# A two-layer encoder: the Fourier branch folded by the symmetry of its channel transform, and the tokens reordered for block copies

## The chip, the cores and the metric

One core of one Trainium2 chip runs the whole kernel in one launch. The metric is the device time of one execution in microseconds (us). The kernel before took 1846.51 us (median of three runs, 1846.41 to 1850.01). Its profile is of one execution whose span, from the first to the last recorded instruction, is 1841.9 us.

## What is computed

Two layers over 512 tokens of 1024 channels, all in float32. Each layer is a SwiGLU half-step, a mixer and a second SwiGLU half-step; the mixer is where the change lies:

```python
# mixer, h = RMSNorm(x)
z = h @ w_in                      # q, k, v (8 heads x 64), uf (512), ga, gf (1024 each)
y_na = neighbourhood_attention(q, k, v, rpb) @ w_na_out
y_f = fourier_mix(uf) @ w_f_out
g_na = jax.nn.sigmoid(ga + gate_bias[0])
g_f = jax.nn.sigmoid(gf + gate_bias[1])
return (g_na * y_na + g_f * y_f) @ w_o

def fourier_mix(u):               # real part of a 2-D DFT, per channel group
    ug = u.astype(jnp.float32).reshape(B, T, F_GROUPS, F_GROUP_DIM)   # 4 groups x 128
    f = jnp.fft.fft2(ug, axes=(1, 3), norm="ortho").real
    return f.reshape(B, T, F_WIDTH).astype(u.dtype)
```

The input of the transform is real. So F(k, c), the result at position frequency k and channel c, equals F(-k, -c), with -k taken modulo 512 and -c modulo 128. The attention sees an 8 x 64 grid of tokens; queries in a block of 16 columns attend to a band of 32 columns in all 8 rows.

## The kernel before, in words

TensorE (PE) multiplies float32 numbers that were split into a high and a low part, each held as fp32r: a product is three matmuls, high by high, high by low and low by high (`mm3`, L326 to L328; `late_low`, L521, L522, L524, for the block products). Weights stream in granules of 128 x 1024 (512 KB). SyncE (SP) issues a load for each (L148); where a granule is the sum of two, either GpSimd (POOL) issues a second, accumulating DMA once the first has landed (L158) or VectorE (DVE) adds the two (L172). ScalarE (ACT) then writes the high part (`whi`; L199, L194, or L179 in `prep_high`) and DVE the low part (`wlo`; L202, L195, L183). The large products are done by Strassen's seven products (`strassen`, `product`), in which a granule feeds twelve matmuls with 512 columns of weights each.

The mixer is `stage_mixer`. It projects u, v, q and k; for the Fourier branch it makes the position transform (`four_pos`), a rotation on DVE (`rotated`), the split of the result (`high_of`), the channel transform (`four_ch`, 24 matmuls for two groups), its assembly into 512 positions (`four_q` on ACT, L1287; `four_y` on DVE, L1292) and its split (`four_high`: ACT L1306, DVE L1310). `rows_of` then multiplies the transform by `w_f_out`: for each of two column halves i and each of four token tiles, four channel groups by three matmuls, 96 in all in a layer. `f_copy` moves a result to SBUF (DVE L1561, once ACT L1559). At the end of the mixer `fill` does the same for the attention's output with `w_na_out`, and the gate blocks begin (`gate_block`, whose first products need the granules that the raw pool opened by `swap_pools(0)` has room for).

Attention goes by eight units (`Probs`, p0 to p7), a head pair and two query blocks each: `att_scores` (PE L1342), `maxes` (DVE L1358), `exps` (ACT L1367), `inverse` (DVE L1370), `scaled` (ACT L1375), `transposed` (PE L1383), `kept` (ACT L1393), `att_pv` (PE L1409), `att_split` (ACT L1418, DVE L1419). The matmuls of the Fourier branch are laid between the units, so that PE works while ACT and DVE do the softmax. In the mixer the order on DVE and ACT is the order in which the code is written (`manual_schedule`), as it stands in the last 150 lines of `stage_mixer`, and the trace shows the instructions of an engine start in that order. The DMA instructions of SP and POOL stand in queues of their own, whose order a scheduler lays down; in the trace they are issued in that order. `minus` (DVE L1548, L1550) and the lines behind it (L1754 to L1769, `t`) prepare the operands of the first gate products.

Of the kernel before, what the change touches and what calls it, by code (L numbers as in the profile page):

```python
# [9 lines left out]
F32 = mybir.dt.float32  # L10
# [24 lines left out]
UNIT = (0, 1, 4, 5, 7, 6, 3, 2)  # L35
KEYS = ((0, 6), (2, 5), (2, 4), (1, 6))

# [5 lines left out]
def _granules():  # L43
# [7 lines left out]
    for l in range(L):  # L51
        for w in (1, 2):
# [15 lines left out]
            if w == 1:  # L68
# [4 lines left out]
                for name, n in (("qk", 8), ("f", 4)):  # L73
                    for g in range(n):
                        put(s, name, g)
# [16 lines left out]
def encoder_kernel(  # L92
# [67 lines left out]
    class Item:  # L160
        def __init__(self, raw, add=None, neg=False, stage=0, parts=1, pieces=1, then=None):
            self.raw, self.add, self.neg, self.stage, self.parts = raw, add, neg, stage, parts
            self.pieces, self.then = pieces, then
# [6 lines left out]
        def summed(self):  # L170
            if self.add:
                V.tensor_tensor(self.raw.t, self.raw.t, self.add.t, ALU.add)  # L172
                self.add = None

        def prep_high(self):

            n, t = self.raw.n, self.raw.t
# [31 lines left out]
    def stage_items():  # L209
# [52 lines left out]
        for l in range(L):  # L262
# [6 lines left out]
            for key in qk[5:] + [(s, "f", g) for g in range(4)]:  # L269
                add(Raw(key))  # L270
            st += 1
# [839 lines left out]
    def stage_mixer(l, norm, nxt):  # L1111
# [5 lines left out]
        ch = mp.tile([P, 2, 2, P], F32R, tag="ch", name=nm("ch"), bufs=1)  # L1117
# [3 lines left out]
        G.dma_start(out=ch, in_=chan)  # L1121
        dfs, rots = [], []
# [13 lines left out]
        def proj_T(scale, ahead=AHEAD, hook=None):  # L1136
            ps = bank()
            wh, wl = ws.next(ahead)
            for kt in range(DT):
# [3 lines left out]
                mm3(ps, wh[:, c], wl[:, c], *xs[kt], kt == 0, kt == DT - 1)  # L1143

            def out(now=True):

                t = tmp(s="q")
                V.tensor_tensor(t, ps, R, ALU.mult)
# [31 lines left out]
        vt = [None] * TB  # L1180

        def value(b, src):
            vt[b] = slot(F32, "v", (T,))
# [93 lines left out]
        def four_ch(b):  # L1277
            bh, bl = b
            p1, p2 = bank(), bank()
            mm3(p1[:, 0:258], ch[:, 0, 0, :], ch[:, 0, 1, :], bh[:, 0:258], bl[:, 0:258], True, True)  # L1280
            mm3(p2[:, 0:256], ch[:, 1, 0, :], ch[:, 1, 1, :], bh[:, 256:512], bl[:, 256:512], True, True)
            return p1, p2

        def four_q(p2):
            qs = tmp(s="fq")
            V.memset(qs[:, 0:1], 0.0)
            S.activation(qs[:, 1:256], p2[:, 1:256], AF.Copy)  # L1287
            return qs

        def four_y(p1, qs):  # L1290
            y = tmp(s="fy")
            V.tensor_tensor(y[:, 0:256], p1[:, 0:256], qs[:, 0:256], ALU.subtract)  # L1292
# [773 lines left out]
```

## Time and profile before

| | before |
|---|---|
| median of the runs | 1846.51 us |
| span of the profiled execution | 1841.9 us |
| around that span, to the median | 4.6 us |
| matrix work (PE) | 1832.5 us busy, 99% of the span |
| DVE busy | 1602.0 us, 87% |
| ACT busy | 1316.5 us, 71% |
| POOL busy | 175.8 us, 10% |
| moved by DMA | 396.77 MB, mean 215 GB/s |

The profile's page counts busy time by engine; a busy PE can be one whose matmuls follow each other without a gap, and 99% says that little time is left in which PE stands. The timeline gives each instruction's start, length, line, output and inputs, with in brackets how long the engine had been idle before it and what released it. The windows view gives the busy time of each engine in a stretch. In the trace the attention of the first layer lies between about 398 and 473 us, that of the second between about 1312 and 1387 us.

### The profile page before, as it was taken

The page shows a single profiled execution, that of the slowest core. Times are in us where ns is not written, and L with a number is a line of the kernel's source. Part 1 is how long each engine was busy: PE and PEld are TensorE (multiplying, and loading weights), DVE is VectorE, ACT ScalarE, POOL GpSimd, SP SyncE. Part 2 cuts the span into 40 slices and gives each one's busy share as a digit, 9 for nine tenths or more (in the row PEclk, how much of TensorE's full clock was granted, in tenths as well). Part 3 has the DMA queues.
Part 4 walks back from the last instruction along what each step waited for, and adds up shares of the span by engine and source line. Part 5 has one row for each costly group of instructions (what it writes and reads, how often), then busy time and mean ns, then how long its engine had stood idle before and what let it go on. Part 6 is the DMA issues. An engine that isn't in the chain of part 4 may idle for free.

```text
span 1841.9 us, 24538 instructions
## 1 busy us (share of the span) xinstructions
PE 1832.5 (99%) x8834; PEld 1528.6 (83%) x8834; DVE 1602.0 (87%) x1942; ACT 1316.5 (71%) x1781; POOL 175.8 (10%) x215
## 2 busy tenths in 40 slices
PE   9999999999999999999999999999999999999998
PEld 7888888888888888888888888888888888888886
DVE  7878899886989988889998888997869899888898
ACT  6777875668676767787667777766686776777865
POOL 0010011100111010001010100101001101010010
PEclk9999999999999999999999999999999999999999
DMA  9898798933887799879888987998258877988795
GB/s 304 224 236 221 186 278 268 227 121 118 238 228 188 157 237 244 215 202 267 250 200 210 237 215 194 280 310 193 69 175 214 231 192 175 230 214 221 206 286 156
DMA packets 202538, 396.77 MB, mean 215 GB/s; under 512 B 108016, under 2 KB 108144, under 8 KB 202416
## 3 DMA queue, kind: packets, MB, share of 16 engines
q1 hardware_dynamic: 173072, 295.28, 51.3%
q0 software_dynamic: 28912, 99.38, 29.5%
q8 instruction: 69, 1.13, 0.2%
q10 hardware_dynamic: 432, 0.55, 0.1%
q14 instruction: 53, 0.43, 0.1%
HBM read 367.88 MB, written 2.11 MB: 201 GB/s over the span
## 4 chain that ended last, share of the span: by engine, by line
PE 99%; DVE 0%; ACT 0%; DMA 0%; issue 0%
PE A L521 10%; PE A L524 10%; PE A L522 10%; PE o L521 8%; PE o L522 8%; PE o L524 8%; PE B L521 5%; PE B L522 5%; PE B L524 5%; PE ps L326 4%; PE ps L327 3%; PE ps L328 3%; PE C L522 3%; PE C L521 3%; PE C L524 3%; PE tr L433 1%
## 5 line engine op out<-in xcount | busy, mean ns | idle before, releaser
L202 DVE TENSOR_TENSOR wlo<-raw,whi 128x1024 fp32r<-128x1024 f32 (+1 forms) x532 | 628.4, 1192 | 168.4 <-ACT whi L199 166.2
L199 ACT ACTIVATE whi<-raw 128x1024 fp32r<-128x1024 f32 (+1 forms) x532 | 545.0, 1034 | 262.3 <-DVE raw L172 56.2
L158 POOL DMA_DIRECT2D raw<-in_wst_dram x166 | 145.3, 901 | 1279.1 <-DMA raw<-in_wst_dram 519.8
L172 DVE TENSOR_TENSOR raw<-raw,raw 128x1024 f32<-128x1024 f32 (+1 forms) x148 | 176.4, 1192 | 2.0
L522 PE MATMUL A<-whi,xl 128*128 128x512 f32 x400 | 155.7, 389 | 0.0
L521 PE MATMUL A<-whi,xh 128*128 128x512 f32 x400 | 155.7, 389 | 0.0
L376 ACT ACTIVATE at<-zt 128x1024 uint16<-128x1024 uint16 (+2 forms) x96 | 110.3, 1166 | 12.7 <-DMA zt<-zs 12.7
L524 PE MATMUL A<-wlo,xh 128*128 128x512 f32 x400 | 115.0, 389 | 0.0
L194 ACT ACTIVATE whi<-raw 128x1024 fp32r<-128x1024 f32 (+1 forms) x83 | 85.6, 1036 | 39.0 <-issue 12.5
L195 DVE SCALAR_TENSOR_TENSOR wlo<-raw,whi 128x1024 fp32r<-128x1024 f32 (+1 forms) x83 | 98.5, 1194 | 16.5 <-ACT whi L194 16.5
L524 PEld LDWEIGHTS A<-wlo,xh 128*128 128x128 f32 x400 | 75.1, 188 | 15.6
L521 PEld LDWEIGHTS A<-whi,xh 128*128 128x128 f32 x400 | 75.1, 188 | 15.4
L522 PEld LDWEIGHTS A<-whi,xl 128*128 128x128 f32 x400 | 75.1, 188 | 15.4
L522 PE MATMUL C<-whi,xl 128*128 128x512 f32 x208 | 81.0, 389 | 0.0
L522 PE MATMUL B<-whi,xl 128*128 128x512 f32 x208 | 81.0, 389 | 0.0
L521 PE MATMUL C<-whi,xh 128*128 128x512 f32 x208 | 80.9, 389 | 0.0
L521 PE MATMUL B<-whi,xh 128*128 128x512 f32 x208 | 80.9, 389 | 0.0
L357 ACT ACTIVATE zs<-th 128x1024 uint16<-128x1024 uint16 x80 | 79.5, 1042 | 1.6 <-DVE th L781 1.6
L774 ACT ACTIVATE th<-sn,rh 128x512 f32<-128x512 f32 x80 | 54.9, 716 | 35.4 <-DVE sn L611 34.6
L606 ACT ACTIVATE sn<-A 128x512 f32<-128x512 f32 x104 | 58.6, 585 | 23.2 <-PE A L524 23.2
L524 PE MATMUL C<-wlo,xh 128*128 128x512 f32 x208 | 59.8, 389 | 0.0
L524 PE MATMUL B<-wlo,xh 128*128 128x512 f32 x208 | 59.8, 389 | 0.0
(436 smaller groups left out, 4687.3 us busy)
## 6 DMA issues: line engine op xcount, KB each, us to landing
raw<-in_wst_dram SPq DMA_DIRECT2D x468, 512.0 KB, 6.0
raw<-in_wst_dram POOLq DMA_DIRECT2D x176, 512.0 KB, 7.9
bm<-in_bias_dram SPq DMA_DIRECT2D x16, 512.0 KB, 4.3
raw<-in_wst_dram SPq DMA_DIRECT2D x30, 256.0 KB, 4.0
x<-in_xin_dram SPq DMA_DIRECT2D x4, 512.0 KB, 10.2
raw<-in_wst_dram POOLq DMA_DIRECT2D x8, 256.0 KB, 8.4
dft<-in_dft_dram POOLq DMA_DIRECT2D x8, 256.0 KB, 11.2
gb<-in_gbias_dram SPq DMA_DIRECT2D x4, 512.0 KB, 9.3
```

The lines of the kernel that those rows point to most:

```text
L158: G.dma_start(out=self.t, in_=wst[GRAN_AT[self.plus]][:, 0 : self.n], accum_op=ALU.add)
L172: V.tensor_tensor(self.raw.t, self.raw.t, self.add.t, ALU.add)
L194: S.activation(hi, t, AF.Copy, scale=-1.0)
L195: self.last = V.scalar_tensor_tensor(lo, t, -1.0, hi.bitcast(F32), ALU.mult, ALU.subtract)
L199: S.activation(hi[:, cs], t[:, cs], AF.Copy)
L202: self.last = V.tensor_tensor(lo[:, cs], t[:, cs], hi[:, cs].bitcast(F32), ALU.subtract)
L326: PE.matmul(ps, lh, rh, start=start, stop=False, skip_group_check=again)
L357: S.activation(s[:, h], words[:, h], AF.Copy)
L376: S.activation(to[:, w], t[:, w], AF.Copy)
L521: PE.matmul(ps, lh, rh, start=start, stop=False, skip_group_check=again)
L522: PE.matmul(ps, ll, rh, start=False, stop=False, skip_group_check=again)
L524: PE.matmul(ps, lh, rl, start=False, stop=stop, skip_group_check=again)
```

## The change

The channel transform is computed for half of the channels, and the mirrored half of the result is made from the first.

- `four_ch` and `four_mid` use plain float32 operands: the rotated values are no longer split, and the transform matrix is one 128 x 164 float32 tile. `four_ch` gives channels 0 to 63 (for two groups, in two column halves of PE) and `four_mid` channel 64 of all four groups (in four 32-column parts). A layer has two calls of `four_ch` and one of `four_mid`: 12 matmuls with 255 to 257 columns in the place of 24 split ones.
- `four_high` writes the high part directly from PSUM in eight-fold strided pieces of 128 columns (four on ACT, four on DVE for the low part); `four_ends` and `ends_split` prepare channel 64.
- `part_f` replaces `rows_of`. The cosine part (m = 0) and the sine part (m = 1) are multiplied apart, for two token tiles in place of four: 6 matmuls of 512 columns a tile and part, and 2 more for channel 64 with m = 0, which makes 56 in a layer in the place of 96. The weights are the sum and the difference of the mirrored halves of `w_f_out`: the sum by an accumulating DMA on POOL, the difference by DVE (`summed`, now with an `op`, and called in `prep_high` too): two such differences in a layer.
- `f_both` makes sum and difference of the two parts (two DVE instructions, in the place of one copy); `f_turn` moves the mirrored rows by eight DMAs on SP for each i (60, 60, 60, 60, 4, 4, 4 and 3 rows); `last_f` and `f_last` make the one row left over: three 32-column float32 matmuls, a copy on DVE, and three POOL DMAs into one row, two of which add to it.
- The tokens are reordered (`_tokens`, `UNIT`) so that mirrored rows stand in blocks. Keys, queries and `att_pv`'s output become strided views, and the value tiles `vs` are built by twelve DMAs of 64 rows a layer (`key_rows`) in the place of four.

```diff
-        def four_ch(b):
...
+        def four_ch(bs):
+
+            ps = bank()
+            for cols, c0, c1 in ((ch[:, 0:64], 0, 257), (ch[:, 64:128], 257, 512)):
+                for e in range(2):
+                    PE.matmul(ps[64 * e : 64 * e + 64, c0:c1], cols, bs[e][:, c0:c1], start=True, stop=True)
+            return ps
...
+        def part_f(m, t, w, i=None):
+
+            ps = bank()
+            c = slice(t * P, (t + 1) * P)
+            for z in range(2):
+                k = slice(z * T, (z + 1) * T)
+                h_, l_ = yf[z][:, 2 * m, c], yf[z][:, 2 * m + 1, c]
+                mm3(ps, h_, l_, w[0][:, k], w[1][:, k], z == 0, z == 1 and m == 1)
+            if m == 0:
+                PE.matmul(ps, e_[:, c], ends[1][i], start=False, stop=False)
+                PE.matmul(ps, e_[:, c], ends[2][i], start=False, stop=True)
+            return ps
...
+        def f_both(i, t, ps):
...
+            f, g = fs[i, t][:, t, :], gs[i][:, t, :]
+            V.tensor_tensor(g, f, ps, ALU.add)
+            V.tensor_tensor(f, f, ps, ALU.subtract)
+
+        def f_turn(i):
+
+            for t, s0, n, tb, d0 in FLIP:
+                nc.sync.dma_start(out=fs[i, tb // 2][d0 : d0 + n, tb % 2, :], in_=gs[i][s0 : s0 + n, t, :])
+
+        def f_last(i, ps):
+
+            t = tmp(s="fl")
+            V.tensor_copy(t[0:96], ps[0:96])
+            to = fs[i, 0][3:4, 1, :]
+            for z in range(3):
+                row = t[32 * z : 32 * z + 1]
+                if z == 0:
+                    G.dma_start(out=to, in_=row)
+                else:
+                    G.dma_start(out=to, in_=row, accum_op=ALU.add)
...
-                f_copy(1, 2, rows_of(yf, 2, second_f))
+                f_both(1, 0, part_f(1, 0, second_f[1]))
                 ts = transposed(p6.s) + transposed(p7.s)
                 swap_pools(0)
...
-                f_copy(1, 3, rows_of(yf, 3, second_f), True)
+                f_both(1, 1, part_f(1, 1, second_f[1]))
                 t12, _ = next(first)
                 po = att_pv(3)
                 ws.prep_high()()
                 att_split(po)
+                f_turn(1)
```

Three places show what this does to the order, two on DVE and one on SP. The names in the rows are tiles with their numbers. The first place is DVE between the softmax of unit p2 and that of p3 (`s` and `nmx` are a unit's scores and row maxima, `rs` the inverse of its row sums, `raw`, `whi` and `wlo` a granule and its two parts); before:

```order
L1358 ISA s_3757,nmx_3758<-ps_3743,bm_3528 128x256
L1358 ISA nmx_3758 128x1
L202 TENSOR_TENSOR wlo_3814<-raw_3232,whi_3813 128x1024
L1370 RECIPROCAL rs_3760<-sm_3759 128x2
L1358 ISA s_3775,nmx_3777<-ps_3761,bm_3526 128x256
```

and after:

```order
L1413 ISA s_3738,nmx_3739<-ps_3724,bm_3515 128x256
L1413 ISA nmx_3739 128x1
L178 TENSOR_TENSOR raw_3353<-raw_3353,raw_3355 128x1024
L209 TENSOR_TENSOR wlo_3791<-raw_3235,whi_3790 128x1024
L1425 RECIPROCAL rs_3741<-sm_3740 128x2
```

The first of the two differences of the Fourier weights now stands between the maxima of p2 and the low part of the granule ahead. The second stands in the same way behind the maxima of p4.

The second place is DVE at the end of the attention (`fs` and `gs` hold the Fourier branch's rows, `t` the operands of the first gate products, `o` the attention's output), from the low part of the first granule for `fill` (`raw_4009` before, `raw_3990` after) to behind that of the second; before:

```order
L202 TENSOR_TENSOR wlo_4267<-raw_4009,whi_4266 128x1024
L1550 TENSOR_TENSOR t_817_4196<-t_817_4196,t_818_4197 128x1024
L183 TENSOR_TENSOR wlo_4303<-raw_4011,whi_4302 128x1024
L1419 TENSOR_TENSOR o_4306<-ps_4285,o_4306 128x512
L195 SCALAR_TENSOR_TENSOR wlo_4316<-raw_4246,whi_4315 128x1024
```

and after:

```order
L209 TENSOR_TENSOR wlo_4243<-raw_3990,whi_4242 128x1024
L1655 TENSOR_TENSOR gs_4195<-fs_4168,ps_4246 128x512
L1656 TENSOR_TENSOR fs_4168<-fs_4168,ps_4246 128x512
L1605 TENSOR_TENSOR t_812_4177<-t_812_4177,t_813_4178 128x1024
L190 TENSOR_TENSOR wlo_4274<-raw_3992,whi_4273 128x1024
L1474 TENSOR_TENSOR o_4277<-ps_4256,o_4277 128x512
```

Two of the four instructions of `f_both` for i = 1 stand between the low part of the first granule and that of the second; the other two stand ahead of the first, where a copy stood. ACT had made the fourth copy before (L1559).

The third place is the queue of SP at the same point. The first two loads are the granules for `fill`, the later ones those of the gate blocks; before:

```order
L148 DMA raw_4009<-in_wst_dram 128x1024
L148 DMA raw_4011<-in_wst_dram 128x1024
L148 DMA raw_4246<-in_wst_dram 128x1024
L148 DMA raw_4248<-in_wst_dram 128x1024
L148 DMA raw_4250<-in_wst_dram 128x1024
L148 DMA raw_4253<-in_wst_dram 128x1024
L148 DMA raw_4256<-in_wst_dram 128x1024
L148 DMA raw_4258<-in_wst_dram 128x1024
L148 DMA raw_4331<-in_wst_dram 128x1024
```

and after, from the first row of `f_turn` for i = 1 on (the two loads for `fill` and the rows of `f_turn` for i = 0 stand ahead of these):

```order
L1661 DMA fs_4168<-gs_4195 60x512 x2
L1661 DMA fs_4166<-gs_4195 4x512
L1661 DMA fs_4166<-gs_4195 3x512
L1661 DMA fs_4166<-gs_4195 60x512
L154 DMA raw_4222<-in_wst_dram 128x1024
L154 DMA raw_4224<-in_wst_dram 128x1024
L154 DMA raw_4226<-in_wst_dram 128x1024
L154 DMA raw_4229<-in_wst_dram 128x1024
L154 DMA raw_4232<-in_wst_dram 128x1024
L154 DMA raw_4234<-in_wst_dram 128x1024
L1661 DMA fs_4166<-gs_4195 60x512
L1661 DMA fs_4168<-gs_4195 4x512 x2
```

The loads of the gate blocks stand behind rows that read `gs` for i = 1. The row of 60 right ahead of the loads reads what the last `f_both` writes. On POOL, the accumulating loads of the gate blocks now stand behind the six DMAs of `f_last` of the layer, of which the second and the third of each i wait for the one ahead to land, since they add to the same row.

265 lines of the change are left out of this document (166 added, 99 removed).

## The prediction

> **What bounds the kernel now.** I read the page first, then the windows of the first layer's attention, then the timelines of PE, ACT, DVE, POOL and SP there. From the page come the span, the busy time and the chain that ended last:
>
> ```profile
> span 1841.9 us, 24538 instructions
> PE 1832.5 (99%) x8834; PEld 1528.6 (83%) x8834; DVE 1602.0 (87%) x1942; ACT 1316.5 (71%) x1781; POOL 175.8 (10%) x215
> PE 99%; DVE 0%; ACT 0%; DMA 0%; issue 0%
> ```
>
> By this PE sets the end, and the other engines cost nothing. But that is an average: it says that PE hardly ever stood, not by how much the others were late to have been waited for. The windows (start and end, then busy time of PE, weight loads, DVE, ACT and POOL, the granted clock, DMA share and GB/s) show it by stage:
>
> ```profile
> 398.00:415.00 17.00, 17.00 (x99) 14.95 (x99) 11.87 (x34) 14.21 (x33) 0.00 (x0) 1.00 0.32 94
> 415.00:432.00 17.00, 17.00 (x115) 14.43 (x115) 14.74 (x40) 16.29 (x40) 0.00 (x0) 1.00 0.37 132
> 432.00:447.00 15.00, 15.00 (x170) 13.33 (x170) 8.49 (x30) 13.18 (x37) 0.00 (x0) 1.00 0.07 28
> 447.00:463.00 16.00, 16.00 (x113) 13.29 (x109) 10.70 (x26) 12.04 (x30) 1.75 (x2) 1.00 0.78 214
> 500.00:520.00 20.00, 20.00 (x90) 16.56 (x89) 20.00 (x23) 13.02 (x14) 2.41 (x3) 1.00 0.74 181
> ```
>
> From 415 to 432 us ACT is busy 16.29 of 17 us, beside a full PE; from 500 to 520 DVE is busy throughout. Here two engines are full at once, and a shorter PE only meets the other. The timelines of ACT, PE and DVE show how near they run (start, length; in brackets the idle time before, and what ended it):
>
> ```profile
> 440.52 1.71 ACT L1375 ACTIVATE s<-s,rs 128x256 f32<-128x256 f32 x4 [1.08 <-DVE rs L1370]
> 454.22 1.71 ACT L1375 ACTIVATE s<-s,rs 128x256 f32<-128x256 f32 x4 [1.71 <-DVE rs L1370]
> ```
> ```profile
> 442.25 1.91 PE L1383 MATMUL ps<-ident,s 128*128 128x128 f32 x16
> 455.95 1.91 PE L1383 MATMUL ps<-ident,s 128*128 128x128 f32 x16
> 462.42 0.50 PE L326 MATMUL ps<-whi,o 128*128 128x512 f32 x1
> 464.14 0.39 PE L327 MATMUL ps<-wlo,o 128*128 128x512 f32 x1
> ```
> ```profile
> 439.73 0.69 DVE L1561 COPY fs<-ps 128x512 f32<-128x512 f32 x1 [3.24 <-PE ps L328]
> 459.62 1.23 DVE L202 TENSOR_TENSOR wlo<-raw,whi 128x1024 fp32r<-128x1024 f32 x1 [1.89 <-ACT whi L199]
> 460.77 1.22 DVE L1550 TENSOR_TENSOR t<-t,t 128x1024 f32<-128x1024 f32 x1
> 462.20 1.22 DVE L183 TENSOR_TENSOR wlo<-raw,whi 128x1024 fp32r<-128x1024 f32 x1 [0.22 <-ACT whi L179]
> ```
>
> ACT ends the last scaling of p5 at 442.23 and of p7 at 455.93; PE begins the transposes that need them at 442.25 and 455.95. These are meetings, not gaps. PE loses nothing, and a shorter PE gains only if ACT comes earlier too. ACT can come somewhat earlier: it stood 1.08 and 1.71 us for DVE's inverses, DVE stood behind a copy in its order, and that copy waited for PE (3.24 us). In `fill`, PE uses the second low part at 464.14; DVE had it ready at 463.42.
>
> **The change part by part: PE.** The rows are one run of 512-column matmuls (first and last of 30), the first of the channel transform and the matmul behind its twelfth, and two calls of `att_pv` from the chain of waits, with the switch behind them:
>
> ```profile
> 449.12 0.39 PE L326 MATMUL ps<-whi,y 128*128 128x512 f32 x1
> ...
> 455.72 0.39 PE L328 MATMUL ps<-whi,y 128*128 128x512 f32 x1
> 398.29 0.28 PE L326 MATMUL ps<-b,ch 128*128 128x258 f32 x1
> ...
> 399.72 0.28 PE L326 MATMUL ps<-dft,u 128*128 128x256 f32 x1
> 436.63 0.50 PE L326 MATMUL ps<-whi,y 128*128 128x512 f32 x1
> 436.97 0.40 PE L327 MATMUL ps<-wlo,y 128*128 128x512 f32 x1
> ```
> ```profile
> 433.06 3.64 PE ps L1409 x64
> ```
>
> A 512-column matmul costs (455.72 - 449.12) / 29 = 0.2276 us; twelve of the channel transform cost 1.43. A layer loses 96 x 0.2276 + 2 x 1.43 = 24.7 us and gains 56 x 0.2276 = 12.7. The float32 matmuls have no row of their own. Nearest is `att_pv`, float32 too and in 64-column halves: 64 records for 32 instructions of 128 columns in 3.64 us, 0.114 us each or 0.89 ns a column. So two `four_ch` (8 x 256 columns) cost 1.9, `four_mid` (4 x 257) 1.0, two `last_f` (6 x 512) 3.0 us with their starts: 5.9. A step of 0.34 us in place of 0.23 behind `att_pv` prices a change of column mode at 0.11; five make 0.5. PE's work falls by 24.7 - 12.7 - 5.9 - 0.5 = 5.6 us a layer, 11 in all. Below, at fp32r's 0.44 ns a column, it falls by 8.5; above, at twice `att_pv`'s price, it rises by 0.3. I take `att_pv`'s price, the same kind of operand in the same kind of column part.
>
> The Trainium skill ("FP8 and Floating Point Precision", TensorE Precision Notes) says that true FP32 takes four passes through the array. For 128 columns four times 0.2276 / 4 would be 0.23 us and the trace has 0.114, in halves that may run side by side; by the rule without overlap the float32 part would be twice 5.9.
>
> **ACT and DVE.** The new steps go by these groups and rows:
>
> ```profile
> L172 DVE TENSOR_TENSOR raw<-raw,raw 128x1024 f32<-128x1024 f32 x140 | 170.9, 1221 | 2.0
> L1561 DVE COPY fs<-ps 128x512 f32<-128x512 f32 x14 | 9.6, 687 | 16.8 <-PE ps L328 16.8
> ```
>
> Back to back they take about 0.08 less (460.77 stands 1.15 behind 459.62). DVE loses the assembly, the splits of the rotated values and half of `four_high`, and gains two differences of weights (1.14 each), four more instructions of `f_both` than copies and the small ones; I count the sum as about zero. What matters is the place:
>
> - The first difference stands ahead of the high part of its granule, which ACT writes before the exponentials of p2. ACT is full there, so p2 and p3 end about 1.2 us later (1.14 and its hand-over). The second stands ahead of p4's inverse, which ACT already waits for. PE's 2.9 us less of channel transform and its shorter `part_f` are mostly waited away here.
> - At p5, ACT regains its 1.08 of idle time, as the copy that DVE stood behind is ready sooner. I put the end of p5's scaling at 442.5 instead of 442.23. PE has done 12 of the 16 transposes by then and gains 1.2 us: of the 1.91 us from 442.25 only the last third is left.
> - At p7 ACT's 1.71 us fall to about nothing; the scaling ends near 454.7, and with six matmuls less behind it PE reaches `fill` at about 458.6 instead of 462.42: 3.8 us early.
> - `fill` takes that back. DVE's low part of the first granule comes about 1.1 us earlier (458.5), but now `f_both` (2 x 0.60), the sum `t` (1.15) and the second low part (1.22) follow: 458.5 + 1.15 + 1.2 + 1.15 + 1.22 = 463.2 in place of 463.42. With the 0.7 us of slack that stood between 463.42 and 464.14, and ACT's copy gone from its queue, I take 463.0 for the use: a gain of 1.1 us. PE stands about 2 us there. If nothing else comes late, 1.1 us a layer is what arrives. Its bounds are 0, if DVE stays where it was, and 3.8, if it is 2.7 us earlier.
>
> **DMA.** These rows carry it: the last copy on DVE ahead of p7's inverse, SP's issues, POOL's first accumulating load, PE's first gate products, and the medians from issue to landing.
>
> ```profile
> 453.43 0.69 DVE L1561 COPY fs<-ps 128x512 f32<-128x512 f32 x1 [0.67 <-PE ps L328]
> 448.74 1.55 SPq L148 DMA_DIRECT2D raw<-in_wst_dram  x3
> 454.96 0.87 POOL L158 DMA_DIRECT2D raw<-in_wst_dram  x1 [89.33 <-DVE rs L1370]
> 473.43 0.39 PE L521 MATMUL A<-whi,xh 128*128 128x512 f32 x1
> 478.87 0.39 PE L521 MATMUL B<-whi,t1h 128*128 128x512 f32 x1
> ```
> ```profile
> raw<-in_wst_dram SPq DMA_DIRECT2D x468, 512.0 KB, 6.0
> raw<-in_wst_dram POOLq DMA_DIRECT2D x176, 512.0 KB, 7.9
> vs<-v SPq DMA_DIRECT2D x8, 128.0 KB, 2.3
> row<-r POOLq DMA_DIRECT2D x5, 2.0 KB, 10.3
> seen<-zt POOLq DMA_DIRECT2D x3, 0.1 KB, 4.1
> dft<-in_dft_dram POOLq DMA_DIRECT2D x8, 256.0 KB, 11.2
> ```
>
> The gate blocks' loads began at 448.74. Now they stand in SP's queue behind the row of `f_turn` that reads the last `f_both`, which ends at about 461: 12 us later. The mirrored rows themselves (120 KB, by `vs` 2.3 us) are not needed until the gates are multiplied in, and hide. At 6.0 us a load, and six of them sharing the engines, I put their landings at 465 to 470, an estimate. The first product needs its first granule at 473.43 - 1.1 = 472.3, with 1.1 us of ACT and 1.2 of DVE to prepare it: by 470, in time. The second product's granules need an accumulating load too (before, the first of these was issued at 454.96): 468 + 7.9 = 476, the high part at 477.1, against 477.8 when PE would begin (478.87 - 1.1); the low part has 1.8 us more (eight matmuls stand ahead). So the cover of 12 us is just used up. With a landing at 470 the wait is 1.2 us; I take 0.4. On POOL these loads follow `f_last`: at `seen<-zt`'s 4.1 us a row (three in a chain from 454, where that copy ends) the way is free at about 463, before the first load has landed. A row of 2 KB lies nearer to it than to `row<-r`, whose 2 KB is gathered by single elements.
>
> The Trainium skill ("DMA: Bandwidth & Descriptors", Anatomy of one DMA, SWDGE path) gives about 2.0 us and bytes over 436 KB/us for such a DMA. That would be 3.2 us for 512 KB where the trace has 7.9, and 2.0 for the row: by it too the chain is done long before.
>
> **The sum.** 1.1 - 0.4 = 0.7 us a layer, 1.4 in all, out of 11 us of PE work. The second layer has the same stages, with the same idle time before the same scalings:
>
> ```profile
> 1354.81 1.71 ACT L1375 ACTIVATE s<-s,rs 128x256 f32<-128x256 f32 x4 [1.08 <-DVE rs L1370]
> 1368.51 1.71 ACT L1375 ACTIVATE s<-s,rs 128x256 f32<-128x256 f32 x4 [1.71 <-DVE rs L1370]
> ```
>
> The profiled execution would go from 1841.9 to 1840.5; with the 4.6 us by which the median lies above its span, 1845.1. Behind the gates the full DVE from 500 on lets little more than 2 us a layer through, even if `fill` were early.
>
> **The rivals.**
>
> - A, faster: the queues of ACT and DVE close up as PE's does, and 3 to 5.5 us a layer arrive: 1835.5 to 1840.5. For it: the 3.24, 1.89 and 1.71 us of idle time above, all released by PE or by what follows PE. Against it: the two added differences, `f_both` ahead of `fill`'s low part, and the full DVE from 500. It is decided by when the second low part of `fill` is ready: with 460.5 or earlier this case holds.
> - B, slower: the chain of three accumulating rows lands by 10.3 us each. The third is issued at 454 + 20.6 = 474.6, the gates' accumulating load after it lands at 483 or later, its high part is there at 484, 6 to 7 us after PE needs it, and one of SP's loads waits for the rows too (485 + 6.0): after the gain, some 7 us a layer, 1859. It decides from about 7 us a row on, where the third row is issued at 468.
> - C, slower: the accumulating loads, now issued among six others, take 11.2 us as the constants' do, not 7.9. The high part is there at 468 + 11.2 + 1.1 = 480.3, 2.5 us late, and the layer loses 1.4 to 1.8: 1849.5. For it: the cover is used up. Against it: the 4 us that separate the two medians belong to another kind of tile.
> - D, slower: the float32 matmuls cost double. PE's work is then as before (+0.3) with the added differences on top, some 1.5 us a layer: also 1849.5. Against it: `att_pv`'s price is measured in column halves, as most of these are.
>
> That the change does not do what it says is excluded by its instruction list: 96 matmuls of 512 columns have become 56.
>
> **How the numbers follow.** Chances: my forecast 0.45, A 0.28, B 0.11, C 0.10, D 0.06. The predicted time is the forecast's, 1845.1; its own range, by 0 to 1.2 us of wait and 0 to 2 us of gain a layer, is 1842.5 to 1848.9. For 8 in 10, I cut off the lower half of A and all of B beyond 1855: 1838 to 1855. About 0.2% (3.7 us) is what a measurement of this kernel can tell from no change. Faster than 1842.8 takes A and a little of the forecast, 0.30; slower than 1850.2 takes B, most of C and half of D, 0.22; 0.48 remains.
>
> **What would show it.** Right: ACT's scaling of p5 at its old place and PE standing ahead of the transposes; PE idle about 2 us in `fill` released by DVE's low part; raw loads issued at about 461; first gate product near 472. Wrong: no idle time of PE in `fill` (A); rows of `f_last` landing after 7 us or more (B); gate products released by a late landing (C); a float32 matmul of 512 columns at 0.9 us (D).

## The result: slower by 1.4%

The changed kernel takes 1874.03 us (median of four runs, 1864.82 to 1877.74), the kernel before 1846.97 (1846.41 to 1850.01): a ratio of 1.0136 (95% interval 1.0108 to 1.0164), 27 us more. Forecast were 1845.1 and a range of 1838 to 1855. The page of the changed kernel:

```profile
span 1875.3 us, 24536 instructions
PE 1834.1 (98%) x8778; PEld 1513.5 (81%) x8778; DVE 1604.9 (86%) x1938; ACT 1305.6 (70%) x1775; POOL 187.5 (10%) x231
PE 88%; DMA 5%; DVE 4%; ACT 1%; issue 1%; SPq 0%; POOL 0%; DVEq 0%; ACTq 0%; POOLq 0%
```

The chain that ended last was PE for 99%; now PE has 88% of it and transfers 5%. The sums of busy time hardly moved (DVE 2.9 us more in all, ACT 10.9 less), so the time went into waiting. The list of PE's waits (total, times, longest) says for what:

```profile
PE A L532 <- ACT sn L617: 17.1, 4, 7.8
PE B L532 <- ACT whi L206: 5.2, 3, 2.7
PE A L532 <- ACT whi L201: 2.7, 2, 1.8
PE ps L1438 <- ACT s L1430: 1.8, 4, 0.5
PE ps L1397 <- DVE o L1474: 1.0, 2, 0.5
```

L532 is the first of the three products of a gate or mixer block (L521 before); all the large waits lie there. The last two rows lie at p5, where the prediction had put a meeting with ACT. The windows (PE, weight loads, DVE, ACT, POOL, clock, DMA share, GB/s), first of the changed kernel, then of the one before:

```profile
447.00:463.00 16.00, 16.00 (x114) 12.36 (x111) 13.76 (x30) 12.63 (x33) 2.02 (x3) 1.00 0.14 42
463.00:480.00 17.00, 13.44 (x58) 10.51 (x57) 10.80 (x11) 6.52 (x9) 2.62 (x3) 1.00 1.02 328
500.00:504.00 4.00, 0.30 (x1) 0.30 (x2) 0.81 (x1) 1.89 (x3) 0.00 (x0) 0.99 1.05 271
504.00:506.00 2.00, 2.00 (x6) 1.53 (x6) 1.79 (x3) 0.80 (x2) 0.24 (x1) 0.50 1.04 270
506.00:508.00 2.00, 2.00 (x8) 1.60 (x7) 2.00 (x2) 1.83 (x2) 0.62 (x1) 0.67 1.04 344
```
```profile
463.00:480.00 17.00, 17.00 (x76) 14.08 (x75) 14.23 (x14) 9.97 (x14) 1.70 (x2) 1.00 0.76 232
```

From 447 to 463 the transfers rest (share 0.14; 0.78 before); from 463 to 512 they are full, and PE, DVE and ACT all do less than before. PE's timeline shows where the layer turns:

```profile
441.77 0.44 PE L1438 MATMUL ps<-ident,s 128*128 128x128 f32 x2 [0.53 <-ACT s L1430]
459.27 1.19 PE L337 MATMUL ps<-whi,o 128*128 128x512 f32 x4
470.28 0.39 PE L532 MATMUL A<-whi,xh 128*128 128x512 f32 x1
474.97 0.50 PE L532 MATMUL A<-whi,xh 128*128 128x512 f32 x1 [1.81 <-ACT whi L201]
479.74 0.50 PE L532 MATMUL B<-whi,t1h 128*128 128x512 f32 x1 [1.75 <-ACT whi L206]
503.70 0.65 PE L532 MATMUL A<-whi,t3h 128*128 128x512 f32 x1 [4.33 <-ACT sn L617]
1478.35 0.79 PE L532 MATMUL A<-whi,t3h 128*128 128x512 f32 x1 [7.81 <-ACT sn L617]
```

The first gate product starts at 470.28 instead of 473.43, though the attention had begun later (its first scores on PE stand at 392.35 instead of 391.10): PE brings 4.4 us to the gates, close to rival A. Then it waits, and behind the gates the layer is 11.3 us late. The issues of SP (start, length, "x" issues in a row), POOL and ACT show why:

```profile
439.76 21.62 SPq L1661 DMA_DIRECT2D fs<-gs  x13
461.49 3.56 SPq L154 DMA_DIRECT2D raw<-in_wst_dram  x6
1461.85 4.94 SPq L374 DMA_TRANSPOSE zt<-zs  x1
```
```profile
453.99 0.51 POOL L1671 DMA_DIRECT2D fs<-fl  x1 [15.93 <-ACT s L1422]
455.82 0.75 POOL L1673 DMA_DIRECT2D fs<-fl  x1 [1.31 <-DMA fs<-fl]
458.05 0.76 POOL L1673 DMA_DIRECT2D fs<-fl  x1 [1.48 <-DMA fs<-fl]
468.86 0.90 POOL L164 DMA_DIRECT2D raw<-in_wst_dram  x1 [10.05 <-DMA raw<-in_wst_dram]
492.98 0.86 POOL L211 DMA_DIRECT2D raw<-in_wst_dram  x1 [6.09 <-DVE wlo L209]
1462.85 0.86 POOL L211 DMA_DIRECT2D raw<-in_wst_dram  x1 [16.80 <-DVE wlo L209]
```
```profile
482.42 1.06 ACT L206 ACTIVATE whi<-raw 128x1024 fp32r<-128x1024 f32 x1 [2.73 <-DMA raw<-in_wst_dram]
502.11 1.06 ACT L206 ACTIVATE whi<-raw 128x1024 fp32r<-128x1024 f32 x1 [4.82 <-DMA raw<-in_wst_dram]
503.07 0.58 ACT L617 ACTIVATE sn<-A 128x512 f32<-128x512 f32 x1
1476.52 1.34 ACT L387 ACTIVATE mq<-zt 128x1024 uint16<-128x1024 uint16 x1 [7.61 <-DMA zt<-zs]
1477.74 0.56 ACT L617 ACTIVATE sn<-A 128x512 f32<-128x512 f32 x1
```

The row of `f_turn` holds SP's queue until 461.4, and the gate loads that began at 448.74 begin at 461.49; the first accumulating load goes out at 468.86 instead of 454.96. The wait that PE shows at 503.70 is two steps away from its cause. PE waits for `sn`, ACT's copy of a full accumulator. That copy stands in ACT's order behind `whi`, which waits 4.82 us for the accumulating load issued at 492.98 (landing 9.0 us later; the median of the accumulating loads from 448 to 500 us was 6.9 before and is 10.4). In the second layer the same copy stands behind `mq`, which waits 7.61 us for a transposing DMA, issued one microsecond ahead of an accumulating load.

### The profile page after: what moved, and what is told of

It reads as the page before. It is cut to its first block, busy times and chain, and to the rows that moved or that the text cites. A ratio compares the mean times of both kernels' runs of the same rounds, so it can differ in the third digit from the quotient of the medians.

```text
span 1875.3 us, 24536 instructions
## 1 busy us (share of the span) xinstructions
PE 1834.1 (98%) x8778; PEld 1513.5 (81%) x8778; DVE 1604.9 (86%) x1938; ACT 1305.6 (70%) x1775; POOL 187.5 (10%) x231
## 4 chain that ended last, share of the span: by engine, by line
PE 88%; DMA 5%; DVE 4%; ACT 1%; issue 1%; SPq 0%; POOL 0%; DVEq 0%; ACTq 0%; POOLq 0%
PE A L532 9%; PE A L535 9%; PE A L533 9%; PE o L535 6%; PE o L532 6%; PE o L533 6%; PE B L533 5%; PE B L535 5%; PE B L532 5%; DMA raw<-in_wst_dram 3%; PE ps L337 3%; PE ps L338 3%; PE ps L339 3%; PE C L532 2%; PE C L533 2%; PE C L535 2%
## 5 line engine op out<-in xcount | busy, mean ns | idle before, releaser
L178 DVE TENSOR_TENSOR raw<-raw,raw 128x1024 f32<-128x1024 f32 (+1 forms) x152 | 181.6, 1195 | 2.0
L532 PE MATMUL A<-whi,xh 128*128 128x512 f32 x400 | 155.9, 390 | 2.7 <-ACT whi L201 2.7
L387 ACT ACTIVATE at<-zt 128x1024 uint16<-128x1024 uint16 (+2 forms) x96 | 110.4, 1168 | 12.3 <-DMA zt<-zs 12.1
L532 PEld LDWEIGHTS A<-whi,xh 128*128 128x128 f32 x400 | 75.1, 188 | 18.9 <-ACT whi L201 3.5
L532 PE MATMUL B<-whi,xh 128*128 128x512 f32 x208 | 81.0, 389 | 0.0
L532 PE MATMUL C<-whi,xh 128*128 128x512 f32 x208 | 81.0, 389 | 0.0
```

The source lines that it names most:

```text
L178: V.tensor_tensor(self.raw.t, self.raw.t, self.add.t, self.op)
L387: S.activation(to[:, w], t[:, w], AF.Copy)
L532: PE.matmul(ps, lh, rh, start=start, stop=False, skip_group_check=again)
```

## The experiments

The theories. **Q**: the gate loads are late because of their place behind `f_turn` in SP's queue, and that lateness is the loss. **Q2**: it is the broken stream of loads that costs. **W**, **D**: work or transferred volume that the change adds. **V**: DVE, with hardly any idle time, sets the pace and can't make up a delay. **T**, formed late: a transposing DMA and an accumulating load hold each other up. The table gives how much later than in the kernel before a profiled execution starts the first gate product and the one behind the gates (473.43 and 539.24 us in the first layer, 1387.72 and 1453.52 in the second); what grows from one column to the next was lost in the gates. The positions are of one execution each, and that of e9 was the fastest of its ten, almost 5 us below the median. Ratios have 95% intervals.

| kernel | time, us | ratio | layer 1: in, behind | layer 2: in, behind |
| --- | --- | --- | --- | --- |
| changed | 1874.03 | 1.0136 (1.0108–1.0164) | -3.2, 11.3 | 11.7, 31.9 |
| e1 loads first | 1866.34 | 1.0110 (1.0094–1.0125) | -4.7, 5.4 | 3.9, 17.5 |
| e2 mirrored rows on POOL | 1861.87 | 1.0071 (1.0044–1.0098) | -3.9, 4.8 | 4.4, 18.6 |
| e3 before, held to 459 | 1851.87 | 1.0027 (1.0015–1.0039) | 0.8, 2.6 | 4.7, 4.7 |
| e4 before, held to 462 | 1863.46 | 1.0095 (1.0080–1.0110) | 0.6, 7.1 | 9.9, 17.2 |
| e5 mirrored rows on ACT | 1852.53 | 1.0038 (1.0023–1.0053) | -3.6, 3.6 | 4.2, 9.2 |
| e6 loads first, `fl` apart | 1863.08 | 1.0098 (1.0078–1.0119) | -4.5, 5.6 | 4.1, 15.7 |
| e7 before, less PE | 1839.24 | 0.9969 (0.9954–0.9983) | -4.8, -4.8 | -6.6, -6.5 |
| e8 nine loads first | 1862.74 | 1.0080 (1.0067–1.0094) | -3.7, 0.3 | 1.2, 15.7 |
| e9 the same, less DVE | 1847.91 | 1.0002 (0.9994–1.0011) | -4.5, -1.3 | -3.9, -1.1 |
| e10 before, more DVE | 1849.70 | 1.0015 (1.0007–1.0024) | 0.6, 0.6 | 5.9, 6.2 |
| e11 changed, plain copies | 1864.88 | 1.0089 (1.0076–1.0101) | -3.0, 9.1 | 7.9, 19.5 |
| e12 before, plain copies | 1847.15 | 1.0000 (0.9992–1.0009) | 0.1, 0.2 | 1.7, 1.8 |
| e13 nine first, plain copies | 1851.51 | 1.0030 (1.0017–1.0043) | -3.2, -0.5 | 0.9, 4.6 |
| e14 changed, turned early | 1865.26 | 1.0090 (1.0076–1.0104) | -1.9, 11.1 | 12.3, 21.0 |
| e15 nine first, turned early | 1854.30 | 1.0036 (1.0023–1.0049) | -3.3, 3.6 | 5.1, 11.5 |

**Loads moved ahead of the mirrored rows (e1, e2, e6).** e1 fixes SP's order so that the loads of `swap_pools` stand ahead of `f_turn(1)`; e2 issues `f_turn(1)` from POOL; e6 is e1 with the tile of `f_last` in a slot of its own.

```diff
-                swap_pools(0)
+                with tc.manual_schedule(engines={mybir.EngineType.SP}):
+                    swap_pools(0)
...
-                f_turn(1)
+                    f_turn(1)
```
```diff
-                nc.sync.dma_start(out=fs[i, tb // 2][d0 : d0 + n, tb % 2, :], in_=gs[i][s0 : s0 + n, t, :])
+                (G if i else nc.sync).dma_start(out=fs[i, tb // 2][d0 : d0 + n, tb % 2, :], in_=gs[i][s0 : s0 + n, t, :])
```
```diff
-            t = tmp(s="fl")
+            t = slot(F32, "fl", (T,))
```

> The changed kernel, with one thing moved: SP's order is fixed at the end of the mixer, so that the six loads of the gate blocks stand ahead of all rows of f_turn for i = 1. Same DMAs, same arithmetic. Theory Q (queue order): the loss is the loads standing 12.7 us behind a DMA that waits for the last f_both. Then the loads are issued near 448 us again, PE keeps the 4.2 us a layer that it had when it reached the gates, and the time is 1836 to 1841. Rival W (work): the loss is from what the change adds to the DMA engines, DVE and ACT around the gates (the mirrored rows, the row sums, the differences). Then order alone does little and the time stays over 1862.

> The changed kernel with the eight rows of f_turn for i = 1 issued by POOL instead of SP, in the order the scheduler gives; SP's loads then stand behind nothing that waits for the last f_both, but POOL's accumulating loads stand behind these rows until about 465 us. Theory Q: near the run with the loads first, 1836 to 1843, since the accumulating loads cannot start before their first loads have landed. Rival W: over 1862. If the accumulating loads' start is what counts and not SP's loads: 1850 to 1865.

> The run with the loads first, with one more thing: the small tile of f_last lies outside the raw pool's space. The fifth of the six loads then no longer waits for the rows of f_last (until about 462 us). The rows of f_turn still stand between the sixth load and the seventh, which cost 10.7 us there. Theory Q2: between the run with the loads first and the unbroken stream, 1853 to 1862. If the wait of the fifth load was all: 1840 to 1849. If it was nothing: 1864 to 1868.

SP's issues in e1:

```profile
451.21 11.48 SPq L154 DMA_DIRECT2D raw<-in_wst_dram  x6
462.80 10.73 SPq L1661 DMA_DIRECT2D fs<-gs  x8
473.79 0.35 SPq L154 DMA_DIRECT2D raw<-in_wst_dram  x1
```

Q's number is missed in both: e1's time lies where W put it, and e2's where a late start of the accumulating loads was to put it. The loads of e1 don't return to 448.74: the first takes the space of a granule that `last_f` reads on PE until about 451, the fifth waited until 461.8, for space of the `fl` tile, and the mirrored rows now hold the later loads from 462.80 to 473.5. In e6 the six loads go out from 451.4 to 454.7, and the seventh still only at 463.5. e6 lies between what Q2 and no effect were to give. Each half of Q's remedy moved the delay to the next transfer: 8 to 12 us of 27 come back.

**The loads held back in the kernel before (e3, e4).** A copy that reads rows of the Fourier output (of its third token tile in e3, of its fourth in e4) stands ahead of the loads on SP's queue; e4 also fixes SP's order there. The computation is unchanged.

```diff
+                back = dp.tile([P, T], F32, tag="back", name=nm("back"))
+                nc.sync.dma_start(out=back[0:60], in_=fs[1, 1][0:60, 0, :])
```
```diff
-                swap_pools(0)
+                with tc.manual_schedule(engines={mybir.EngineType.SP}):
+                    swap_pools(0, False)
...
+                    back = dp.tile([P, T], F32, tag="back", name=nm("back"))
+                    nc.sync.dma_start(out=back[0:60], in_=fs[1, 1][0:60, 1, :])
+                    ws.enter(ws.stage + 1)
```

> The kernel before, with one DMA added on SP ahead of the gate blocks' loads: it writes 60 rows of the Fourier result to a scratch in DRAM that nobody reads, and waits for the third copy of i = 1, at about 457.7 us, so the loads are issued 9 us later than before. Theory Q: the gates follow their loads with 2 to 3 us of slack, so 6 to 7 us a layer are lost: 1858 to 1861. The prediction's cover (12 us of it were to be used up before PE waits): no loss, 1846 to 1848. Rival W: no loss either, since none of the change's work is here.

> As the run before it, but the added DMA waits for the fourth copy of i = 1 (about 461 us), so the loads are issued 12.5 us later than before. Theory Q: 9 to 10.5 us a layer lost, 1865 to 1868, and the step from the run held 9 us is about as long as the added delay (3.5 us a layer). The prediction's cover: 0 to 1.2 us a layer, 1846.5 to 1849. Rival W: no loss.

SP in e4, then PE's waits there:

```profile
461.84 0.40 SPq L1748 DMA_DIRECT2D back<-fs  x1
462.40 5.32 SPq L148 DMA_DIRECT2D raw<-in_wst_dram  x9
```
```profile
PE A L521 <- ACT sn L606: 4.8, 2, 2.5
PE B L521 <- ACT whi L199: 3.8, 3, 1.9
```

This is the pair that carries Q, though both times lie below Q's numbers. With nothing of the fold, loads 10.4 us late (459.17) cost 5.0 us, 1.9 of them in the gates, and loads 13.7 us late cost 16.5, 13.8 of them there, with the same two waits at the same products as in the changed kernel. W isn't needed for such a loss. So the cover is some 9 us, not 12, and beyond it a microsecond of delay costs more than one: 3.3 us later is 11.6 us dearer over two layers. The changed kernel's loads are 12.7 us late, and PE comes 4.4 us earlier on top. In the first layer the first load leads the first gate product by 24.7 us before, 15.1 in e3, 11.6 in e4 and 8.8 in the changed kernel.

**Does PE's gain survive at all? (e7)** In the kernel before, 24 matmuls a layer are left out: the low part of `w_f_out` in three of the four token tiles.

```diff
+                if src is yf and tb:
+                    PE.matmul(ps, h_[:, t], wh[:, c], start=kt == 0, stop=False)
+                    PE.matmul(ps, l_[:, t], wh[:, c], start=False, stop=kt == 3)
```

> The kernel before, without the matmuls that multiply the low part of w_f_out in three of the four token tiles: 24 matmuls of 512 columns a layer fewer, 5.5 us of PE work, which is what the fold takes away net; nothing else is changed, so that part of the product is left out. If PE's work alone sets the end: 1835 to 1837. By the prediction's meetings with ACT and DVE, 1 to 2 us a layer arrive: 1842 to 1845. Rival D and theory Q2 say that the gates' loads (issued as before) take back what PE gains beyond their lead: 1842 to 1848, with waits of PE in the gates.

The 4.8 us that PE gains before the gates of the first layer are still there behind them, and none of it is waited away: with the loads in time, neither ACT nor DVE takes the gain back. Of 48 x 0.2276 = 10.9 us of work the median shows 6.6; the second layer adds only 1.7.

**One stream of loads (e5, e8).** Both take `fl` out of the way and call `last_f(1)` earlier; e5 then issues `f_turn(1)` from ACT, e8 from SP behind nine loads.

```diff
-                nc.sync.dma_start(out=fs[i, tb // 2][d0 : d0 + n, tb % 2, :], in_=gs[i][s0 : s0 + n, t, :])
+                (nc.scalar if i else nc.sync).dma_start(out=fs[i, tb // 2][d0 : d0 + n, tb % 2, :], in_=gs[i][s0 : s0 + n, t, :])
```
```diff
+                    if i == 0:
+                        with tc.manual_schedule(engines={mybir.EngineType.SP}):
+                            f_turn(1)
...
+                pl = last_f(1, raw)
                 pf = [part_f(0, t, second_f[0], 1) for t in range(2)]
                 second_f.append(ws.next(0))
-                pl = last_f(1, raw)
```

> The changed kernel with three things moved so that nothing of the Fourier branch stands in the way of the gate blocks' loads: f_turn for i = 1 is issued by ACT, the small tile of f_last lies in a buffer that is not in the space of the raw pool, and last_f for i = 1 stands ahead of the two part_f (so its granule is free 3.6 us sooner). Theory Q2 (a broken load stream): the loads run from about 447 to 450 us on, the 7th to 9th and the gate biases follow without a gap, and the time is 1840 to 1849. Rival D (volume): the gates are fed at the DMA engines' rate, so PE's early arrival is waited away and the time is 1847 to 1853 even so. Rival W (DVE and ACT work around the gates): over 1858.

> The unbroken stream without its side effect: f_turn for i = 1 is again issued by SP, but behind nine loads of the gate blocks, so that ACT is not held up (in the run before it stood 7 us at the start of the gates and PE waited 4.28 and 2.95 us for it). The tile of f_last and the place of last_f stay as there. Theory Q2 (broken stream, now whole): PE keeps most of the 3.6 to 4.2 us a layer with which it reaches the gates: 1838 to 1843. Rival V (DVE sets the pace through the gates): in the changed kernel DVE ends the second low part for fill at 463.4 us, exactly where it does before, so the gates can end no earlier than before, and PE's early arrival is waited away: 1844 to 1849.

ACT in e5:

```profile
460.56 6.23 ACTq L1661 DMA_DIRECT2D fs<-gs  x7
466.83 1.06 ACT L1856 ACTIVATE t1h<-t 128x1024 fp32r<-128x1024 f32 x1 [6.98 <-DMA fs<-gs]
```

Issuing is not free: seven issues keep ACT from computing for 6.2 us, and PE pays 4.28 us for it in the first gate product. The granted clock is then 0.50 to 480 and 0.68 to 484, some 2.8 us more (an estimate from these two windows); after that PE waits no longer in this layer's gates. So e5, whose time lies where D put it, does not tell D from ACT's waits. e8 was to free ACT and came out slower than any of its forecasts. Its first layer's gates lose 4.0 us instead of 14.4. The second layer still loses 14.5, and half of that is a single wait of 7.34 us:

```profile
1446.54 5.01 SPq L374 DMA_TRANSPOSE zt<-zs  x1
```
```profile
1447.54 0.86 POOL L211 DMA_DIRECT2D raw<-in_wst_dram  x1 [17.24 <-DVE wlo L209]
```
```profile
1460.74 1.34 ACT L387 ACTIVATE mq<-zt 128x1024 uint16<-128x1024 uint16 x1 [7.14 <-DMA zt<-zs]
```

The loads are in time and ACT waits for something else: a transposed tile that lands 14 us after its issue. In the trace of the kernel before, transposes take 5.1 us in the median and 8.1 at most.

**The transposing DMA (e11, e12, e13, e14, e15).** In e11 to e13 the transposing DMAs between the gates become plain copies of the same bytes, in the changed kernel, the one before and e8. In e14 and e15 the transposition stays, and the later of two is called for with the first, in the changed kernel and in e8.

```diff
+    def unturned(z):
+        s, t = words_apart(z), slot(U16, "zt", (2, 4, 256))
+        nc.sync.dma_start(out=t.rearrange("p h q t -> p (h q t)"), in_=s.rearrange("p h q b f -> p (h q b f)"))
+        return t
...
-            turned[j] = apart(ga0[j])
+            turned[j] = unturned(ga0[j])
```
```diff
-            1, bias, acts, {1: lambda: taken(1), 5: lambda: taken(0), 2: lambda: channels(1), 7: lambda: channels(0)}
+            1, bias, acts, {1: lambda: (taken(1), taken(0)), 2: lambda: channels(1), 7: lambda: channels(0)}
```

> The changed kernel, in which the three transposing DMAs a layer between the gates (zt from zs) are plain copies of the same 512 KB, so that the words are not turned; all instructions else are the same. In the changed kernel the second layer's last long wait (7.81 us at the first product with t3h) ends with ACT, whose reading of zt (mq) waits 7.61 us for the transpose issued at 1461.85, one microsecond ahead of an accumulating load. Theory T (transpose and accumulating load hold each other up): with plain copies this wait falls to under 3 us and the 4.33 us wait of the first layer changes by less than 1.5; the time falls by 5 to 9 us, to 1865 to 1869. Theory Q alone (the transfers are late whatever their kind): the wait stays above 5 us, the time within 3 us of 1874.

> The control: the kernel before with the same three plain copies a layer in place of the transposing DMAs. There no transpose was waited for between the gates, so by T and by Q alike the time stays within 3 us of 1846.5; what it gains is to be taken off what the other two kernels of this call gain.

> The kernel of the run with nine loads first (1862.74), in which the first layer lost almost nothing and the second kept one 7.34 us wait for the same reading of zt, with the three plain copies a layer. T: that wait goes and with it about 6 to 7 us: 1855 to 1857. Q alone: 1860 to 1863.

> The changed kernel, with the whole computation, in which the second transposing DMA between the gates (of the first token half's sums) is called for together with the first, at the second gate's first product instead of its second: ahead of one weight load on SP's queue and, by T, clear of the accumulating load that is issued one microsecond behind it now. T: the reading of zt no longer waits 7.6 us in the second layer; the time falls by 4 to 9 us, to 1865 to 1870. If the order of the issues doesn't matter and the two kinds of transfer only share the engines, the wait moves with it and the time stays within 3 us of 1874.

> The same in the kernel with nine loads first (1862.74). T: the 7.34 us wait goes; 1853 to 1858, with the whole computation still made. Otherwise 1860 to 1864. Neither is expected to beat the kernel before (1846.5): the added work of DVE, 4.7 us a layer, stays.

SP, POOL and ACT in e14, at the place of the 7.61 us wait, and PE's longest waits in e13:

```profile
1460.61 3.04 SPq L374 DMA_TRANSPOSE zt<-zs  x1
```
```profile
1462.35 0.87 POOL L211 DMA_DIRECT2D raw<-in_wst_dram  x1 [15.70 <-DVE wlo L209]
```
```profile
1468.04 1.36 ACT L387 ACTIVATE mq<-zt 128x1024 uint16<-128x1024 uint16 x1
```
```profile
PE A L538 <- ACT sn L623: 3.2, 2, 1.8
PE ps L1444 <- ACT s L1436: 2.4, 6, 0.5
```

T holds as far as the transposition goes. Without it (the words are then not turned) the changed kernel gains 9.2 us and e8 11.2, more than expected (5 to 9, and 6 to 7), and the control gains nothing. With it, but called for earlier (1.7 us ahead of the accumulating load instead of 1.0, and in e15 1.5 us), they gain 8.8 and 8.4: the tile is there when ACT comes for it (no idle time at 1468.04), and SP's issue takes 3.0 us, not 4.9. The four runs of the changed kernel spread over 13 us, so the two differences from e8 are the surer ones. So the transposition's kind and its place in the order cost time.

That the accumulating load is the other party is inferred from the issue times; no run moved that load alone. In the changed kernel, e1, e2, e6 and e8 the two are 1.0 to 1.3 us apart at nine places, and ACT waits for the tile at each: 7.61 and 7.14 us at two of them, 1.1 to 2.7 at the others. At 1.5 us and more it doesn't wait, but for the second layer of e2, with 7.29 us at 1.65. So the distance alone doesn't set the price, and how two transfers slow each other is not shown.

**DVE (e9, e10).** e9 leaves 4.7 us of DVE's added work a layer out of e8 (the subtraction in `f_both` and the differences of the weights); e10 adds five copies of 0.60 us a layer to the kernel before.

```diff
-                V.tensor_tensor(self.raw.t, self.raw.t, self.add.t, self.op)
+                if self.op is ALU.add:
+                    V.tensor_tensor(self.raw.t, self.raw.t, self.add.t, self.op)
...
-            V.tensor_tensor(f, f, ps, ALU.subtract)
```
```diff
+            for _ in range((tb >= 2) + by_act):
+                V.tensor_copy(to, ps)
```

> The run with the nine loads first, without part of the work on DVE: the subtraction in f_both (four instructions of 0.60 us a layer) and the differences of the Fourier weights (two of 1.14) are left out, 4.7 us a layer, so the mirrored sums and the sine part are not the reference's. Rival V: DVE comes 2 to 4.7 us a layer sooner to the gates and the time falls by 4 to 9 us against the run with the nine loads first. Theory Q2 alone: within 2 us of it.

> The kernel before, with DVE copies repeated where f_both has its instructions (five of 0.60 us a layer: one each behind the third copies and the first fourth copy, two behind the last, which ACT makes). Output is the same; loads and PE's work are untouched. Rival V: the gates begin later by what DVE is later than its slack, 1.5 to 3 us a layer: 1848 to 1852. Theory Q2 alone: 1846 to 1847.

e9 comes 14.8 us below e8, but no long wait for a transposed tile is left in it, so part of this is T again; against e13 and e15, which have lost that wait too, it is 3.6 and 6.4 us. e10 costs 3.0 us for 6 us of copies. V is real and small: DVE's share is some 4 to 6 us.

**What it adds up to.** The transposition's place: 8.8 us (changed to e14). The loads' place in the queue and the space that they wait for: 11.0 (e14 to e15). DVE's work in its new places: 6.4 (e15 to e9). Together 26.1 of 27.1; the terms are differences between whole kernels, and in another order they would divide somewhat differently. The sum explains only the way back to the kernel before. e9 still has the shorter PE, which alone was worth 6.6 us in e7, and is no faster than the kernel before: its gates still lose some 3 us a layer, and that is not taken apart. Q2 and D weren't tested apart from Q. No kernel with the fold's whole computation beat the one before; e5 and e15 came nearest, 0.4% slower. The layers also drift by 1 to 5 us elsewhere (e12 comes to the second layer 1.7 us late at an unchanged median, e10 5.9). In part that is the reference: in every later run the time is the span plus 1.7 to 1.9 us, so the profiled execution of the kernel before (span 1841.9) took about 1843.7, less than any of its four runs. The rest is not explained, and no reading here rests on so little.

## Why the prediction was wrong

- **PE's work**: right. The 4.4 us at the gates and 1.4 us of waits at p5 make 5.8, where 5.6 was forecast. The float32 part was rather too dear: the three matmuls of one `last_f` (two records each) take 0.99 us in the chain of waits where 1.5 was forecast, 0.33 us a matmul, so rival D is out:

```profile
451.72 0.99 PE ps L1642 x6
```

- **p5**: right. PE stands there for ACT's scaling, 0.53 and 0.36 us, then 0.51 for DVE.
- **`fill`**: wrong. PE reaches it at 459.27 (forecast: about 458.6), and DVE's second low part is ready at 463.49, in the first row below (463.0). But PE doesn't wait there. The changed program has four products of the high part first and uses that low part only in its twenty-second matmul, 4.9 us later (the last row). I had carried over the old order of PE. The term "a gain of 1.1 us" measured 4.4:

```profile
462.27 1.22 DVE L190 TENSOR_TENSOR wlo<-raw,whi 128x1024 fp32r<-128x1024 f32 x1
479.72 1.23 DVE L209 TENSOR_TENSOR wlo<-raw,whi 128x1024 fp32r<-128x1024 f32 x1 [3.36 <-ACT whi L206]
483.51 1.23 DVE L209 TENSOR_TENSOR wlo<-raw,whi 128x1024 fp32r<-128x1024 f32 x1 [2.56 <-ACT whi L206]
```
```profile
464.16 0.39 PE L338 MATMUL ps<-wlo,o 128*128 128x512 f32 x1
```

- **The cap behind the gates**: "the full DVE from 500 on lets little more than 2 us a layer through" is wrong as a limit. In e7, 4.8 us came to the first layer's gates and 4.8 came out behind them.

- **The chain of `f_last`**: right that it hides, too dear in price. Its rows are 1.8 to 2.2 us apart, not 4.1, and rival B is out. The Trainium skill ("DMA: Bandwidth & Descriptors", Anatomy of one DMA, SWDGE path), which gives 2.0 us for so small a transfer, was nearer than the row I took. With the loads in flight beside them, in e5 and e8, a row takes 3.9 to 5.4 us to land.
- **The DMA term**: this is the step that failed: "So the cover of 12 us is just used up. With a landing at 470 the wait is 1.2 us; I take 0.4." The loads are issued where forecast, at 461.49. The cover measures about 9 us (e3, e4), and PE's earlier arrival uses 4 more of it. Three things were not in the term. The loads pushed together make each other and the accumulating loads slower (in e4's trace the nine land 4.4 to 15.5 us after their issues; in the changed kernel the accumulating ones go from 6.9 to 10.4), for the whole stage and not only for the first product. DVE's waits (3.36 and 2.56 us above) fall ahead of a stage in which it is full, so they are hardly made up; this is argued, not shown apart. And an accumulator's copy stands behind a waiting `whi` on ACT, so PE waits for a granule that its own product doesn't use. Rival C had part of the mechanism and a price of 1.4 to 1.8 us a layer; the gates lose 14.4 in the first layer.
- **Not in the prediction at all**: the transposing DMA beside an accumulating load, 9 us. In the kernel before (SP, then POOL) the same two are issued 2.5 us apart. That the delay of the loads alone brought them together is not so: in e8, with the loads in time, they are 1.0 to 1.2 us apart, and in e9, with less DVE work, 2.5 again:

```profile
1438.64 3.00 SPq L363 DMA_TRANSPOSE zt<-zs  x1
```
```profile
1441.11 0.86 POOL L204 DMA_DIRECT2D raw<-in_wst_dram  x1 [15.39 <-DVE wlo L202]
```

- **Rival A** had PE's gain right and the sign of the outcome wrong: the gain reached the gates and was lost there.

## What to carry to other kernels

When a change puts one queued transfer ahead of others, price the whole stage behind it and not only the first consumer: move every later issue by the same delay, and ask at each whether its landing, under full transfer engines, still precedes the work that shares its consumer's queue. A shorter PE makes that cover thinner by just what it gains. And where a program is ordered by a scheduler, read the order of the changed program at each place where a wait is forecast, before the wait is put into a sum.

## What the runs showed of the hardware

- After the 4.33 us wait the granted clock is 0.50 from 504 to 506 and 0.67 to 508, where PE gets through 14 matmuls instead of the 21 of full speed before: about 1.6 us more for one wait. After the waits of 1.75 and 1.81 us it stays at 1.00 (475 to 483). The Trainium skill ("TensorE: Matmul & The Clock Gate", What's actually happening) has the array fall to half rate after an idle window of about 3.4 us; as a limit for a single wait the traces don't bear that out. In the changed kernel's second layer the clock is 0.50 from 1408.9 to 1411 after a wait of 2.69 us, and in e4 0.50 from 482.5 to 484.5 after one of 1.86, while after 2.58 us at 545.8 in the changed kernel it stays at 1.00.
- The tile of a transposing DMA, which lands after 5.1 us in the median of the kernel before, came 14 us after the issue at three places (changed kernel, e2 and e8, second layer), with an accumulating load issued 1.0 to 1.7 us behind it; at seven others with 1.0 to 1.3 us it came after 8 to 10.
- Transfers issued from ACT cost ACT 0.9 us each (6.23 for seven in e5) in which it doesn't compute.
